# Layer 0 keeps the split projection weights of the first half in DRAM for the second half

## The chip, the cores and the metric

The kernel runs on one core of one Trainium2 chip. The metric is device time in microseconds (us) from the start to the end of one execution. Engines are named as in the profile: PE is TensorE, DVE is VectorE, ACT is ScalarE, POOL is GpSimd, SP is SyncE, which here issues nearly all transfers.

## The reference

The reference is a trunk of two layers over a sequence of 1024 steps and 1024 channels in float32. Layer 0 mixes with two head groups (RWKV-7, and a gated DeltaNet "gdn"), layer 1 with chunked attention; each layer then has an MLP and a gated embedding. The change touches only the input projection of layer 0:

```python
h = rmsnorm(x, norm_mix_g[i])
proj = h @ even_w_in[e]                     # 1024 x (3*512 + 4*512 + 8)
y_a, v_first = rwkv7_group(h, dh, proj[..., :o_ak], ...)   # r, k, v
y_b = gdn_group(proj[..., o_bq:o_bg], ...)                  # q, k, v, gate, two logits
mix = jnp.concatenate([y_a, y_b], -1) @ even_w_out[e]
```

## The kernel before

**Products in three parts.** A float32 product is made of three products in the format float32r: each operand is split into a high part (a cast by ScalarE, line L306) and a low part (a subtraction by VectorE, L307), and `mm3` multiplies high by high, high by low and low by high. One projection of 128 output channels for half of the sequence (512 steps) takes eight k-tiles, so 24 products of 128x512, written to a PSUM bank called `dps` and scaled out of it by VectorE (L684, L709 for LoRA).

**Weights.** The 28 blocks of the projection's weights (512 KB each) lie in `w_in`. `load_w` takes a raw buffer (tag `wraw`, two buffers), loads a block into it (L300, on SP's queue), and `split_w` splits it into a pair `whi`, `wlo` (two pairs). So a block may be loaded when the split before the last is done, and be split when the projection before the last has been multiplied.

**Units and lanes.** Layer 0 goes through the sequence in two halves (`hf` 0 and 1), each with eight units: four pairs of RWKV heads and four gdn heads in turn. A unit takes three weight blocks (RWKV) or four (gdn, the fourth is the gate). Each half begins with further products: the decay LoRA before the first unit's projections in the second half, and after the first unit the logits (`gdn_logits`, L719 and L720: a memset by GpSimd of a raw buffer, a small load, a split) and the gate LoRA (`lora`, L695 to L713). These use the same raw buffers and pairs.

Seven generators ("lanes") emit the instructions: the input lane `l0_in` makes projections, others the fronts (RWKV or gdn: VectorE, ScalarE and GpSimd work, then the start of a triangular inverse), the mids (the end of the inverse, banks `iz`), the backs (the recurrence over chunks, banks `ch`, `py`, `po`, `pm`) and the posts. A planner with a table of latencies chooses the lane that goes next; the projections fill the time in which the others wait. It counts products only, no loads and no splits. The order within an engine's queue is settled when the program is built, by when each instruction's operands and buffers are expected, and on the chip each queue is taken in order.

**The inverse's way through memory.** `inverse_start` stores a block matrix to DRAM (L399), loads it in another layout (L403), runs some 30 small operations on GpSimd (L411 to L421), stores the result (L423) and loads it again (L425). All four are on SP's queue, among the weight loads.

Of the kernel before, what the change touches and what calls it, by code (L numbers as in the profile page):

```python
# [8 lines left out]
F32 = mybir.dt.float32  # L9
F32R = mybir.dt.float32r  # L10
# [7 lines left out]
P = 128  # L18
T = 1024
# [93 lines left out]
class Trunk:  # L113
# [456 lines left out]
    def l0_in(self, units):  # L570
        nc, a, fr = self.nc, self.a, self.fr
        self.state = {}
        self.xg = []
        for u, (nm, p, hf) in enumerate(units):
            if u % 8 == 0:


                self.xg, squares = [], []
                if hf == 0:
                    acc = fr.tile([P, HB], F32, tag="rsbc", name="acc", bufs=2)  # L580
                    raw = self.wp.tile([P, 1024], F32, tag="wraw", name="wraw")
                    self.w_first = [self.wp.tile([P, 1024], F32R, tag=f"w{q}", name=f"w{q}") for q in ("hi", "lo")]
                    first = iter([slice(0, HB), slice(HB, T)])
                else:

                    x2 = [self.load_x(q, self.pre if q < 2 else self.wp, "ph" if q == 0 else "pl" if q == 1 else "wraw")
                          for q in range(4)]
                for k in range(NK):
                    if hf == 0:
                        if k % 2 == 0 and k < 4:  # L590
                            c = next(first)
                            nc.sync.dma_start(out=raw[:, c], in_=a["w_in"][4][:, c])
                            self.split_w(raw[:, c], HB, [z[:, c] for z in self.w_first])
                        xr = self.t2()
                        (nc.sync if k > 1 else nc.scalar).dma_start(out=xr, in_=a["x"][k, :, 0:HB])
                    else:
                        xr = x2[k // 2][:, k % 2, :]
                    if k % 2 == 0:
                        xg2 = self.pair(k // 2)
                    xg = xg2[:, k % 2]  # L600
                    self.split_scaled(xg, xr, self.vec("mixg", k), slice(0, HB))
                    self.xg.append(xg)
                    if hf == 0:
                        squares.append(lambda k=k, xr=xr: self.square(acc, xr, k == 0))
                for f in squares:
                    f()
                sc = {}
                if hf == 0:
                    rsc = self.sm.tile([P, 4], F32, tag="rsc", name="rsc")
                    self.rs = fr.tile([P, HB], F32, tag="rsbc", name="rsbc", bufs=2)  # L610

                    self.extra = [lambda t=t: self.psm.tile([P, HB], F32, tag=t, name="dps") for t in ("y", "ch", "pm")]
                    self.late, self.plan = [], {2: lambda: self.row_stats([acc], rsc), 3: lambda: self.to_rows(rsc, self.rs)}
                    raws = yield from getattr(self, nm + "_in")(p, hf, u)
                    self.wa2 = fr.tile([P, 512], F32, tag="wa2", name="wa2")
                    nc.sync.dma_start(out=self.wa2, in_=a["wa2"])
                    self.g2 = self.l0.tile([P, 512], F32, tag="g2", name="g2")
                    nc.sync.dma_start(out=self.g2, in_=a["g2"])
                    self.hv = self.l0.tile([P, 2, 4], F32, tag="hv", name="hv")
                    nc.sync.dma_start(out=self.hv.rearrange("p a b -> p (a b)"),  # L620
                                      in_=a["gdnhv"].rearrange("(o c) -> o c", o=1).broadcast_to((P, 8)))
                    self.ea = self.l0.tile([P, 1, 4], F32, tag="ea", name="ea")
                    nc.scalar.activation(self.ea, self.hv[:, 0:1, :], AF.Exp)
                    acc = fr.tile([P, HB], F32, tag="rsbc", name="acc", bufs=2)
                    for q in range(4):
                        x2 = self.load_x(q, self.pre, "pl" if q % 2 else "ph")
                        for e in range(2):
                            self.square(acc, x2[:, e], q + e == 0, nc.vector)
                else:
                    self.rs = acc  # L630
                self.pst = None
                sc["lwa"] = yield from self.lora(0, [(0, 64, 0), (64, 128, 1)], "la")
                nc.scalar.activation(sc["lwa"][0:64], sc["lwa"][0:64], AF.Tanh)
            if u:
                raws = yield from getattr(self, nm + "_in")(p, hf, u)
            self.state[u] = (raws, sc)
            self.mark(("in", u), 1.0)
            if u == 7:
                rsc = self.sm.tile([P, 4], F32, tag="rsc", name="rsc")
                self.row_stats([acc], rsc)  # L640
                yield "l0_in1"
                self.to_rows(rsc, acc)
            if u % 8 == 0:

                ba = yield from self.gdn_logits()
                gg = yield from self.lora(1, [(0, 128, 2)], "lg", lambda: self.gdn_scalars(hf, sc, ba))
                nc.scalar.activation(gg, gg, AF.Tanh, scale=0.5)
                nc.vector.tensor_scalar(gg, gg, 0.5, 0.5, op0=ALU.mult, op1=ALU.add)
                sc["lg"] = gg
                self.mark(("lg", hf))  # L650

        rsb = lambda: fr.tile([P, HB], F32, tag="rsbc", name="xs", bufs=2)
        pt = [self.pair(k) for k in range(2)]
        sc = [self.pair(q, F32) for q in (2, 3)]
        sc = [t[:, e] for t in sc for e in range(2)]
        yield from self.ple_proj(0, lambda k, hf: pt[k][:, hf], sc[0], lambda n: sc[1 + n % 3], rsb, self.load_w)
        yield from self.out_early(0, a["x"], self.pair, rsb, self.load_w, [("post", 7), ("post", 13), ("post", 14), ("post", 15)])
# [111 lines left out]
    def gdn_cum(self, sc):  # L769
# [16 lines left out]
        nc.scalar.activation(sc["ekd"], gl, AF.Exp)  # L786
        nc.scalar.activation(sc["egl"].rearrange("p i h -> p (i h)"), pc[:, 16:32], AF.Exp)

    def rwkv_in(self, p, hf, u):
        raws = []  # L790
        for j in (1, 0, 2):
            if u >= 2:
                yield ("raw", u - 2, j)
            w = self.load_w(self.a["w_in"][4 * j + p]) if u or j != 1 else self.w_first
            raws.append((yield from self.project(w, f"r{p}{j}", 1)))
        return [raws[1], raws[0], raws[2]]

    def gdn_in(self, n, hf, u):
        raws = []
        for j in (1, 0, 2):  # L800
            if u >= 2:
                yield ("raw", u - 2, j)
            raws.append((yield from self.project(self.load_w(self.a["w_in"][12 + 4 * j + n]), f"g{n}{j}", 3)))
        if u >= 4:
            yield ("front", u - 2)
        gate = yield from self.project(self.load_w(self.a["w_in"][24 + n]), None, 0, "gate")
        return [raws[1], raws[0], raws[2], gate]

    def rwkv_front(self, p, hf, sc, raws, u):
# [1376 lines left out]
```

## Time and profile before

| | us |
|---|---|
| median of 3 runs | 3078.52 |
| lowest and highest run | 3070.69, 3079.13 |
| the profiled execution, whole | 3086.63 |
| its span, first to last instruction | 3084.8 |
| its mean granted TensorE clock | 0.974 of full |

The profile's page gives busy time by engine, then the span in 40 slices, the DMA queues, the chain that ended last, and the costliest groups of instructions, as line, engine, operation, output<-input, count, busy time and mean, and the idle time before them with its releaser. The windows view gives the same busy times for chosen stretches. In the timeline the first two columns are start and duration in us; a bracket at the end holds the idle time of the engine before it and what ended it. A row `A <- B: t, n, m` of the waits says that A waited for B for t us in all, n times, at most m us.

The first half of layer 0 lies at about 0 to 415 us of the span, the second at about 415 to 790 us.

### The profile page before, as it was taken

To read this page: it belongs to the slowest core of one execution; us is meant where nothing else is said; L and a number is where in the kernel's file an instruction comes from. 1 tells how busy PE (TensorE), PEld (TensorE's weight loads), DVE (VectorE), ACT (ScalarE), POOL (GpSimd) and SP (SyncE) were. 2 spreads that over 40 slices of the span, in tenths; PEclk is the share of its full clock that TensorE was granted. 3 is DMA by queue.
4 is the path that set the end of the run, shared out by engine and by line. 5 is a ranking of instruction groups with operands and counts; after the bars stand their busy time and mean duration, and the time that the engine had idled before them with its cause. 6 is when DMAs were issued, how large, how long until landed. Compare 5 with 4: busy or idle time off the path is not lost.

```text
span 3084.8 us, 47290 instructions
## 1 busy us (share of the span) xinstructions
PE 2970.1 (96%) x17254; PEld 2457.1 (80%) x17254; DVE 2209.9 (72%) x4546; ACT 1486.2 (48%) x2957; POOL 552.9 (18%) x985
## 2 busy tenths in 40 slices
PE   8999999999999999999999999999999999999999
PEld 6777777777777888788887988898878888888887
DVE  7556766667758777788887676676768777788883
ACT  4333433434437555544444465565757555544441
POOL 5434442443500000000005111111210000000002
PEclk9899999999999999999999999999999999999999
DMA  4212112212346444754424211110256444654433
GB/s 145 64 55 62 54 49 75 61 55 68 110 157 227 162 150 151 262 166 151 151 95 131 70 44 40 43 61 23 75 181 223 163 154 153 237 190 150 150 103 116
DMA packets 194857, 368.49 MB, mean 119 GB/s; under 512 B 46800, under 2 KB 49088, under 8 KB 194624
## 3 DMA queue, kind: packets, MB, share of 16 engines
q1 hardware_dynamic: 163808, 309.35, 31.4%
q10 hardware_dynamic: 30816, 56.11, 4.7%
q8 instruction: 136, 2.23, 0.3%
q14 instruction: 97, 0.79, 0.1%
HBM read 268.86 MB, written 96.53 MB: 118 GB/s over the span
## 4 chain that ended last, share of the span: by engine, by line
PE 71%; DVE 14%; DMA 6%; ACT 4%; issue 2%; POOL 1%; SPq 0%; ACTq 0%; DVEq 0%; POOLq 0%
PE dps L180 57%; PE ch L180 2%; PE po L180 2%; DVE act L1283 2%; PE pm L180 1%; PE iz L180 1%; PE pt L195 1%; DMA late<-in_w 1%; PE sn L180 1%; PE tp L180 1%; DMA late<-hd 1%; DVE late L1431 1%; DMA wraw<-in_w_out 1%; PE py L180 1%; DVE wlo L307 1%
## 5 line engine op out<-in xcount | busy, mean ns | idle before, releaser
L180 PE MATMUL dps<-r,act 128*128 128x512 f32 x3720 | 872.9, 392 | 2.0 <-DVE xw L1550 0.8
L180 PEld LDWEIGHTS dps<-r,act 128*128 128x128 f32 x3720 | 698.0, 188 | 157.0 <-issue 1.2
L180 PE MATMUL dps<-xg,whi 128*128 128x512 f32 x1280 | 436.0, 421 | 11.2 <-ACT whi L306 7.4
L1647 POOL TENSOR_TENSOR pn<-pn,prs 128x512 f32<-128x512 f32 x32 | 47.3, 1483 | 1542.6 <-ACT prs L389 1419.5
L180 PE MATMUL dps<-wq,act 128*128 128x384 f32 x1536 | 307.8, 347 | 13.8 <-DVE vs L1909 6.0
L180 PEld LDWEIGHTS dps<-xg,whi 128*128 128x128 f32 x1280 | 236.2, 197 | 62.2 <-ACT whi L306 7.6
L180 PEld LDWEIGHTS dps<-wq,act 128*128 128x128 f32 x1536 | 269.6, 193 | 17.7 <-DVE vs L1909 7.6
L180 PE MATMUL dps<-xg,wlo 128*128 128x512 f32 x640 | 260.7, 407 | 2.6 <-DVE wlo L307 2.6
L1282 ACT CAST act<-act 128x512 fp32r<-128x512 f32 (+2 forms) x281 | 159.3, 600 | 142.0 <-PE dps L180 59.8
L1283 DVE TENSOR_TENSOR act<-act 128x512 fp32r<-128x512 f32 (+2 forms) x281 | 180.1, 669 | 4.6 <-ACT act L1282 4.6
L180 PE MATMUL dps<-act 128*128 128x512 f32 x720 | 176.5, 393 | 2.0 <-DVE late L1404 2.0
L1282 ACT CAST act<-late 128x512 fp32r<-128x512 f32 x210 | 123.7, 620 | 100.4 <-PE dps L180 73.8
L180 PE MATMUL dps<-late,act 128*128 128x512 f32 x672 | 166.6, 392 | 0.0
L180 PEld LDWEIGHTS dps<-act 128*128 128x128 f32 x720 | 136.2, 189 | 32.1 <-DVE late L1404 2.4
L1283 DVE TENSOR_TENSOR act<-late,act 128x512 fp32r<-128x512 f32 x210 | 139.1, 687 | 31.1 <-ACT act L1282 30.9
L180 PEld LDWEIGHTS dps<-xg,wlo 128*128 128x128 f32 x640 | 125.0, 195 | 32.5 <-DVE wlo L307 3.8
L180 PEld LDWEIGHTS dps<-late,act 128*128 128x128 f32 x672 | 126.0, 188 | 27.7
L180 PE MATMUL dps<-xw,act 128*128 128x512 f32 x576 | 145.9, 392 | 0.2 <-ACT act L1282 0.2
L1550 DVE TENSOR_TENSOR xw<-xw,dps 128x512 f32<-128x512 f32 x192 | 130.0, 682 | 17.3 <-PE dps L180 17.2
L306 ACT CAST whi<-wraw 128x1024 fp32r<-128x1024 f32 (+1 forms) x79 | 81.8, 1035 | 107.6 <-PE dps L180 77.1
L180 PEld LDWEIGHTS dps<-xw,act 128*128 128x128 f32 x576 | 107.9, 188 | 24.4 <-ACT act L1282 0.7
L180 PE MATMUL po<-ptile,vs 128*128 128x256 f32 (+1 forms) x576 | 106.8, 295 | 15.5 <-ACT ptile L352 9.7
(488 smaller groups left out, 5600.7 us busy)
## 6 DMA issues: line engine op xcount, KB each, us to landing
hb<-late ACTq DMA_DIRECT2D x196, 256.0 KB
act<-hb SPq DMA_DIRECT2D x158, 256.0 KB
late<-in_w SPq DMA_DIRECT2D x60, 512.0 KB
act<-in_w SPq DMA_DIRECT2D x112, 256.0 KB
wraw<-in_w_in SPq DMA_DIRECT2D x55, 512.0 KB
braw<-hb SPq DMA_DIRECT2D x80, 256.0 KB
wraw<-in_w_out SPq DMA_DIRECT2D x21, 512.0 KB
wraw<-in_w_qkv SPq DMA_DIRECT2D x21, 512.0 KB
```

The lines of the kernel that those rows point to most:

```text
L180: return self.begin(self.nc.tensor.matmul(out, lhsT, rhs, start=start, stop=stop, skip_group_check=again))
L195: return self.begin(self.nc.tensor.transpose(out, in_, ident))
L306: nc.scalar.copy(hi, raw)
L307: nc.vector.tensor_tensor(lo, raw, hi.bitcast(F32), op=ALU.subtract)
L1282: A.copy(hi, s)
L1283: V.tensor_tensor(lo, s, hi.bitcast(F32), op=ALU.subtract)
L1431: V.tensor_tensor(t, u, v, op=ALU.subtract)
L1550: V.tensor_tensor(x[n][:, hs[hf]], x[n][:, hs[hf]], ps, op=ALU.add)
L1647: G.tensor_tensor(pn, pn, prs[:, sl], op=ALU.mult)
```

## The change

In the first half `load_in` loads and splits each block as before, and then stores its high and low part to DRAM (two stores of 512 KB on SP's queue, into the tensors `wd`). The block that the kernel splits ahead of everything (`w_first`, block 4) is stored within `l0_in`. In the second half `load_in` loads both parts in place of the raw block; there is no split. Two of three blocks go into the `whi`, `wlo` pairs, and every third into the two raw buffers (`nw % 3 == 2`), which no projection's raw block needs in that half. The loads wait on nothing but a free buffer and the stores of the first half. LoRA, logit and all later weights are loaded and split as before.

```diff
     def l0_in(self, units):
...
+        self.wd, self.nw = {}, -1
...
                             self.split_w(raw[:, c], HB, [z[:, c] for z in self.w_first])
+                            if k == 2:
+                                self.wd[4] = [self.dr.tile([P, T], F32, tag=f"wd4{q}", name="wd") for q in "hl"]
+                                for d, z in zip(self.wd[4], self.w_first):
+                                    nc.sync.dma_start(out=d, in_=z.bitcast(F32))
...
+    def load_in(self, o, hf):
+
+        nc = self.nc
+        if hf == 0:
+            hi, lo = w = self.load_w(self.a["w_in"][o])
+            self.wd[o] = [self.dr.tile([P, T], F32, tag=f"wd{o}{q}", name="wd") for q in "hl"]
+            for d, z in zip(self.wd[o], w):
+                nc.sync.dma_start(out=d, in_=z.bitcast(F32))
+            return w
+        self.nw += 1
+        if self.nw % 3 == 2:
+            w = [self.wp.tile([P, T], F32R, tag="wraw", name="w" + q) for q in ("hi", "lo")]
+        else:
+            w = [self.wp.tile([P, T], F32R, tag=f"w{q}", name=f"w{q}") for q in ("hi", "lo")]
+        for d, z in zip(self.wd[o], w):
+            nc.sync.dma_start(out=z.bitcast(F32), in_=d)
+        return w
+
     def rwkv_in(self, p, hf, u):
...
-            w = self.load_w(self.a["w_in"][4 * j + p]) if u or j != 1 else self.w_first
+            w = self.load_in(4 * j + p, hf) if u or j != 1 else self.w_first
...
     def gdn_in(self, n, hf, u):
...
-            raws.append((yield from self.project(self.load_w(self.a["w_in"][12 + 4 * j + n]), f"g{n}{j}", 3)))
+            raws.append((yield from self.project(self.load_in(12 + 4 * j + n, hf), f"g{n}{j}", 3)))
...
-        gate = yield from self.project(self.load_w(self.a["w_in"][24 + n]), None, 0, "gate")
+        gate = yield from self.project(self.load_in(24 + n, hf), None, 0, "gate")
```

## The prediction

> **What bounds the kernel now.** I read the page first, then the busy time of each engine in the two halves of layer 0, then the groups of instructions in the second half, the waits of TensorE there, and the timelines around TensorE's gaps.
>
> ```profile
> span 3084.8 us, 47290 instructions
> PE 2970.1 (96%) x17254; PEld 2457.1 (80%) x17254; DVE 2209.9 (72%) x4546; ACT 1486.2 (48%) x2957; POOL 552.9 (18%) x985
> PEclk9899999999999999999999999999999999999999
> ```
>
> TensorE is busy for 96% of the span, so what this change can win is idle TensorE time and time at a lowered clock, and only where the removed work stood: the second half of layer 0, about 415 to 790 us. The windows view gives those stages (microseconds; busy time and count of PE, PEld, DVE, ACT, POOL; then the granted clock, the DMA share and GB/s):
>
> ```profile
> 77.00:410.00 333.00, 319.09 (x2747) 245.67 (x2746) 208.69 (x464) 126.35 (x262) 141.47 (x320) 0.93 0.21 60
> 415.00:790.00 375.00, 360.78 (x3070) 278.07 (x3069) 240.67 (x568) 144.30 (x308) 154.78 (x360) 0.96 0.20 61
> 10.00:15.00 5.00, 4.37 (x16) 3.16 (x15) 4.11 (x6) 5.00 (x10) 4.80 (x11) 1.00 1.04 400
> 450.00:455.00 5.00, 5.00 (x56) 3.70 (x55) 4.28 (x10) 0.00 (x0) 3.19 (x7) 0.50 0.14 58
> ```
>
> In the second half TensorE stands idle for 375 - 360.78 = 14.2 us, and a clock of 0.96 over 375 us loses another 15 us. So 29 us (0.95% of the span) is the most that can be won there, if every stall went.
>
> **What is removed.** The 28 projection weights of the second half lose a ScalarE cast and a VectorE subtraction each. The groups of instructions by line in that stage (busy us, mean ns, idle before and its cause; 32 and 31 because LoRA and logit weights are split there too, and stay so):
>
> ```profile
> L307 DVE TENSOR_TENSOR wlo<-wraw,whi 128x1024 fp32r<-128x1024 f32 x31 | 39.4, 1272 | 3.5 <-ACT whi L306 3.4
> L306 ACT CAST whi<-wraw 128x1024 fp32r<-128x1024 f32 x32 | 33.5, 1046 | 34.7 <-PE dps L180 32.0 <-DMA wraw<-in_w_ple 2.3 <-POOL subt L418 0.3
> ```
>
> That is 28 x 1.272 = 35.6 us of VectorE and 28 x 1.046 = 29.3 us of ScalarE, and most of the 32.0 us in which ScalarE stood at a cast until TensorE released a buffer. But neither engine is the bound. What TensorE waits for there, and its larger gaps (last bracket: idle time, releaser):
>
> ```profile
> PE pm L180 <- DVE PMQ L942: 5.4, 3, 2.9
> PE tp L180 <- DVE b L875: 2.9, 2, 1.5
> 449.66 1.65 PE L180 MATMUL pm<-AR,b 64*128 64x128 f32 x4 [2.03 <-DVE PMQ L942]
> 573.04 1.16 PE L180 MATMUL tp<-AR,b 64*128 64x128 f32 x16 [1.40 <-DVE b L875]
> 576.20 1.62 PE L180 MATMUL pm<-AR,b 64*128 64x128 f32 x4 [1.07 <-POOL subt L418]
> 664.92 1.22 PE L180 MATMUL pm<-AR,b 64*128 64x128 f32 x3 [2.90 <-DVE PMQ L942]
> 761.12 1.16 PE L180 MATMUL tp<-AR,b 64*128 64x128 f32 x16 [1.52 <-DVE b L875]
> ```
>
> These four places make 8.9 of the 14.2 us, and no wait for a projection's weights is among them. Each is the RWKV front's own VectorE chain. VectorE ahead of the last gap, and the one split that stands ahead of the first:
>
> ```profile
> 757.90 1.58 DVE L901 SCALAR_TENSOR_TENSOR f<-f,vecs 128x512 f32<-128x512 f32 x1
> 759.40 0.68 DVE L684 TENSOR_TENSOR raw<-dps,acc 128x512 f32<-128x512 f32 x1
> 760.00 1.06 DVE L875 TENSOR_TENSOR b<-f 128x512 f32<-128x512 f32 x1
> 762.06 1.21 DVE L307 TENSOR_TENSOR wlo<-wraw,whi 128x1024 fp32r<-128x1024 f32 x1
> 444.74 1.20 DVE L307 TENSOR_TENSOR wlo<-wraw,whi 128x1024 fp32r<-128x1024 f32 x1
> ```
>
> At 761 the split comes after the operation awaited; the one at 444.74 belongs to the gate LoRA, which keeps its split. So the relief is far nearer to nothing than to 29: bounds 0 and -29 us. I take **-3 us**, a tenth, for shorter VectorE queues elsewhere.
>
> **What is added in steady state.** A second-half load is now two transfers of 512 KB each into the buffers that the products read. I price it by SyncE's issue, the 400 GB/s of the window 10:15 above, and the longest wait for a small transfer to land:
>
> ```profile
> wraw<-in_w_in SPq DMA_DIRECT2D x55, 512.0 KB
> L300 SPq DMA_DIRECT2D wraw<-in_w_in x55: 327/333/530, 6.6 to 738.4; - x55
> SPq L425 <- DMA z<-sub: 11.2, 8, 2.4
> SPq L399 <- DVE b L1119: 53.1, 5, 17.0
> ```
>
> 1.05 MB at 400 GB/s is 2.6 us; with 0.33 us of a second issue and 2.4 us it is 5.3 us from release to use. There are three buffer pairs (two of their own, and the raw pair for every third weight), so weight n may load once projection n-3 has been multiplied, and must be there when n-1 has. VectorE's evictions show the ends of projections; the two shortest such spans I found:
>
> ```profile
> 475.57 0.69 DVE L709 TENSOR_TENSOR lgo<-dps,acc 128x512 f32<-128x512 f32 x1 [0.15 <-PE dps L180]
> 485.65 0.69 DVE L684 TENSOR_TENSOR raw<-dps,acc 128x512 f32<-128x512 f32 x1 [0.15 <-PE dps L180]
> 513.57 0.69 DVE L684 TENSOR_TENSOR raw<-dps,acc 128x512 f32<-128x512 f32 x1 [8.55 <-PE dps L180]
> 523.43 0.69 DVE L684 TENSOR_TENSOR gate<-dps,acc 128x512 f32<-128x512 f32 x1 [1.92 <-PE dps L180]
> ```
>
> They are 10.1 and 9.9 us long, so a load of 5.3 us is covered, unless SyncE then stands at a wait of its own: it stood at the store that starts an inverse (L399) for up to 17.0 us. A load caught behind all of that is late by 17.0 + 5.3 - 9.9 = 12.4 us. I take **0**, upper end +12. The wait for the pair itself moves from ScalarE to SyncE; behind it there stand later loads and the stores and loads of the inverse.
>
> In the first half, SyncE gets two stores behind each split. They become ready at the moment when the load after next does (that load waits for the same split), so they add two issues (0.66 us), no new long wait. Their 28 x 1.05 = 29.4 MB take 73 us at 400 GB/s out of 333, so the DMA share goes from 0.21 to about 0.43. An inverse goes through memory in four hops (store, load, store, load): 8 x 4 hops, each meeting stores with a chance of about 0.2 and then waiting half of 2.6 us on average, make 8 us in all. No row of TensorE's waits above names a transfer, so I take **+1**, ends 0 and +8. The stores can't speed the first half up, as nothing is taken from it.
>
> **At the start** the transfers are saturated (share 1.04 above), and the first LoRA load is the next thing due:
>
> ```profile
> 18.41 0.34 SPq L695 DMA_DIRECT2D lraw<-in_lora  x1
> 24.45 2.05 POOL L703 TENSOR_TENSOR wraw<-lraw,d_omul 128x512 f32<-128x512 f32 x2
> 26.54 1.05 ACT L306 CAST whi<-wraw 128x1024 fp32r<-128x1024 f32 x1 [6.57 <-POOL wraw L703]
> ```
>
> Issued at 18.41, it needs 2.4 + 1.3 us, so it is there by 22.1, and GpSimd uses it at 24.45. Three stores ahead of it (1.57 MB, 3.9 us) would make that 26.0: 1.6 us late. I take **+0.5**, ends 0 and +2.
>
> **Between the halves.** The logit weights (L719) use a raw buffer. It used to be free as soon as a split was done; now the third projection of the first second-half unit holds both raw buffers until its last product. GpSimd, SyncE, TensorE and VectorE there:
>
> ```profile
> 419.01 0.94 POOL L719 MEMSET wraw<- 128x1024 f32 x1
> 419.98 0.60 SPq L720 DMA_DIRECT2D wraw<-in_wba  x1
> 423.78 0.50 POOL L411 TENSOR_SCALAR_AFFINE_SELECT sub<-subb 32x256 f32<-32x256 f32 x1 [3.70 <-DMA subb<-scr]
> 437.20 0.65 POOL L421 COPY sub<-sub 32x256 f32<-32x256 f32 x1
> 441.76 0.62 PE L180 MATMUL dps<-xg,whi 128*128 128x512 f32 x2
> 442.86 0.69 DVE L684 TENSOR_TENSOR raw<-dps,acc 128x512 f32<-128x512 f32 x1
> 443.33 0.25 PE L180 MATMUL iz<-T,Ng 32*32 32x16 f32 x8
> ```
>
> The third projection is evicted at 442.86, its buffers come free at about 442. Memset 0.94, issue 0.60, landing 2.4, cast 1.05 and subtraction 1.27 follow: 6.3 us, to about 448.3. The logit products began at 441.76. If TensorE keeps its order it waits 6.3 us; the gap of 2.03 us at 449.66 then goes, since VectorE catches up meanwhile: 4.3 us. A halved clock comes on top: behind the 2.03 us gap TensorE ran at 0.50 for 5 us, which costs 2.5 us. That gives +6.8. If the inverse and recurrence products are put ahead of the logits instead, the 2.03 us gap takes up the logits and it costs nothing. Queue orders are set when the program is built, by when operands are expected, so the second is likely in part: **+3**, ends 0 and +7.
>
> The Trainium skill ("TensorE: Matmul & The Clock Gate", Part 1) says that the clock halves after an idle window of about 3.4 us. The row 450:455 differs: 2.03 us idle was enough. By the page shorter waits would cost no clock, the half-way value would be 2 rather than 3, and the sum below +0.5.
>
> **Sum.** -3 + 0 + 1 + 0.5 + 3 = **+1.5 us**. The profiled execution took 3086.6 us (span 3084.8), 8 us over the median of 3078.5; so 3088.1 for it and **3080.0** beside the median. With ends that rarely meet, this case spans about -8 to +9 us.
>
> **Rivals.** *Slower, the memset in GpSimd's way.* GpSimd takes its queue in order. If the memset keeps its place ahead of the inverse's operations (419.01 before 423.78), the inverse starts after about 443 and not at 423.78: 19 us late. TensorE's first inverse product, at 443.33, then waits about 19 us, less the 2.03 us gap: +17, so 3080 - 3 + 17 = 3094. It decides if L719 stands ahead of L411 in GpSimd's queue. For it: that order is there now. Against: the memset's readiness is known when the order is made. *Slower, the hops.* All 8 us of waiting hops show: 3080 + 7 = 3087, with a late load or the start's upper end 3090. The Trainium skill ("DMA: Bandwidth & Descriptors", Queues, rings and completion order) says that each DMA engine takes one queue's work in ring order, which is this rival's mechanism; no run here shows it yet. Against it: no TensorE wait for a transfer. *Faster.* Freed ScalarE and VectorE shorten the recurrence, and half of the 29 us goes: -14.5 + 4.5 = -10, 3068.5. For it: ScalarE's 32.0 us at the casts. Against: no gap above has a removed split in front of it.
>
> **How the numbers follow.** A measurement of this kernel can tell about 0.3% (9 us) from no change. Forecast 0.44, which lies within 0.3%; memset 0.18, slower; hops and late loads 0.18, about the bound, of which I count 0.15 slower and 0.03 same; faster 0.20. So faster 0.20, same 0.47, slower 0.33. The range runs from 3066 (a little beyond the faster case) to 3098 (the memset case with a late start); 0.2 is left out. The forecast's own range is 3072 to 3089.
>
> **What would show it.** Casts at L306 in the second half fall from 32 to 4, and ScalarE's wait at them from 32 us to little; the four gaps stay; written bytes rise by 29 MB, the first half's DMA share to about 0.43; L719 starts at 442 or later. I am wrong if the RWKV front's gaps go (faster), if GpSimd waits at L719 with the inverse behind it, or if TensorE waits for a weight's transfer (slower).

## The result

| | before | after |
|---|---|---|
| median (runs) | 3076.15 us (22) | 3068.52 us (22) |
| lowest and highest run | 3067.63, 3085.11 | 3055.84, 3075.47 |
| the profiled execution, whole | 3086.63 | 3072.22 |
| its span | 3084.8 | 3070.2 |
| its mean granted TensorE clock | 0.974 | 0.980 |

The ratio is 0.9976 [0.9966, 0.9986]: 7.6 us between the medians, 7.4 by the ratio. The interval excludes no change, so the kernel is a little faster; the size stays inside the 0.3% that the prediction had named. The spans of the two profiled executions lie 14.6 us apart, twice the medians' difference, so differences of single profiles are read with care below.

The page of the kernel after, its heads:

```profile
span 3070.2 us, 47342 instructions
PE 2960.9 (96%) x17254; PEld 2448.3 (80%) x17254; DVE 2167.2 (71%) x4518; ACT 1459.8 (48%) x2929; POOL 540.4 (18%) x985
HBM read 283.54 MB, written 125.89 MB: 133 GB/s over the span
```

VectorE lost 28 instructions (4546 to 4518) and 42.7 us of busy time, ScalarE 28 and 26.4 us. The windows of the first and the second half (columns as in the prediction):

```profile
77.00:410.00 333.00, 317.46 (x2695) 244.42 (x2694) 205.13 (x460) 124.15 (x257) 141.05 (x319) 0.92 0.39 134
415.00:790.00 375.00, 365.99 (x3206) 282.47 (x3199) 213.84 (x567) 122.72 (x291) 140.44 (x360) 0.99 0.33 104
```

In the second half TensorE is idle for 375 - 365.99 = 9.0 us, where it was 14.2, and its clock is 0.99, where it was 0.96. The first half gained nothing. (A window of fixed time holds more work in the faster kernel, 3206 products and not 3070; a stretch of fixed work follows with the table of all runs.) Groups by line in the second half, and what TensorE waits for there:

```profile
L307 DVE TENSOR_TENSOR wlo<-wraw,whi 128x1024 fp32r<-128x1024 f32 x5 | 6.1, 1225 | 3.6 <-ACT whi L306 3.6
L306 ACT CAST whi<-wraw 128x1024 fp32r<-128x1024 f32 x5 | 5.2, 1046 | 7.5 <-POOL wraw L708 3.6 <-DMA z<-sub 1.3 <-PE dps L180 1.0
```

```profile
PE tp L180 <- DVE b L898: 2.2, 2, 1.4
PE ch L180 <- ACT W L997: 1.9, 1, 1.9
PE dps L180 <- ACT whi L306: 1.5, 2, 0.9
PE pm L180 <- DVE PMQ L965: 0.9, 1, 0.9
```

The casts are gone but for five, and with them ScalarE's 32.0 us of waiting for TensorE in front of them (1.0 is left). The wait for `PMQ` fell from 5.4 to 0.9 us. No wait for a weight's transfer has come in its place. TensorE's larger gaps there (last bracket: idle time, releaser):

```profile
451.60 0.73 PE L180 MATMUL dps<-xg,whi 128*128 128x512 f32 x2 [0.60 <-ACT whi L306]
570.26 0.66 PE L180 MATMUL ch<-W,F 128*128 128x64 f32 x4 [1.94 <-ACT W L997]
571.77 2.08 PE L180 MATMUL tp<-AR,b 64*128 64x128 f32 x16 [0.85 <-DVE b L898]
656.70 0.92 PE L180 MATMUL pm<-AR,b 64*128 64x128 f32 x4 [0.89 <-DVE PMQ L965]
749.33 1.16 PE L180 MATMUL tp<-AR,b 64*128 64x128 f32 x16 [1.40 <-DVE b L898]
```

The largest gap of before, 2.90 us at 664.92, is 0.89 us here. VectorE's timeline shows why, before and then after:

```profile
659.16 1.76 DVE L874 SCALAR_TENSOR_TENSOR AR<-f,E 128x512 f32<-128x512 f32 x1
660.84 1.75 DVE L818 SCALAR_TENSOR_TENSOR f<-raw,vecs,f 128x512 f32<-128x512 f32 x1
662.70 1.70 DVE L901 SCALAR_TENSOR_TENSOR f<-f,vecs 128x512 f32<-128x512 f32 x1
664.32 0.54 DVE L942 TENSOR_TENSOR PMQ<-pm,mask 128x384 f32<-128x384 f32 x1
```

```profile
654.42 1.76 DVE L897 SCALAR_TENSOR_TENSOR AR<-f,E 128x512 f32<-128x512 f32 x1
656.10 0.55 DVE L965 TENSOR_TENSOR PMQ<-pm,mask 128x384 f32<-128x384 f32 x1
656.76 1.10 DVE L841 SCALAR_TENSOR_TENSOR f<-raw,vecs,f 128x512 f32<-128x512 f32 x1
```

Before, `PMQ` stood in VectorE's queue behind two operations of 1.75 and 1.70 us; after, it stands right behind `AR`. No split was taken out between them: the queues were written in another order when the program was built. TensorE's queue holds some 14,800 matrix instructions; set side by side as the programs are built, the two written orders differ in some 1,500 lines (buffer numbers left out; a row that moved counts twice, also where the expectations below speak of rows), some 340 of them in layer 1, more than half in its attention, which the change does not touch.

So there are two theories. **Engine time**: 28 x 1.27 us of VectorE and 28 x 1.05 us of ScalarE less in the second half let the queues serve TensorE earlier, in whatever order they are written. **Order**: any edit makes a new order, and this one came out well.

### The profile page after: what moved, and what is told of

Read it like the earlier page. It is cut to its first block, busy times and chain, and to the rows that moved or that the text cites. A ratio compares the mean times of both kernels' runs of the same rounds, so it can differ in the third digit from the quotient of the medians.

```text
span 3070.2 us, 47342 instructions
## 1 busy us (share of the span) xinstructions
PE 2960.9 (96%) x17254; PEld 2448.3 (80%) x17254; DVE 2167.2 (71%) x4518; ACT 1459.8 (48%) x2929; POOL 540.4 (18%) x985
## 4 chain that ended last, share of the span: by engine, by line
PE 76%; DVE 11%; DMA 5%; ACT 3%; POOL 2%; issue 2%; SPq 0%; ACTq 0%; DVEq 0%; POOLq 0%
PE dps L180 62%; PE ch L180 2%; PE po L180 2%; PE iz L180 1%; PE pt L195 1%; PE pm L180 1%; PE tp L180 1%; PE sn L180 1%; DVE act L1306 1%; DMA late<-hd 1%; DMA wraw<-in_w_qkv 1%; PE py L180 1%; DVE ptile L353 1%; PE pp L180 1%; DVE pb L2047 0%
## 5 line engine op out<-in xcount | busy, mean ns | idle before, releaser
L180 PE MATMUL dps<-xg,whi 128*128 128x512 f32 x1280 | 429.5, 416 | 12.7 <-ACT whi L306 8.9
L1573 DVE TENSOR_TENSOR xw<-xw,dps 128x512 f32<-128x512 f32 x192 | 130.1, 682 | 18.3 <-PE dps L180 18.0
L180 PEld LDWEIGHTS po<-ptile,vs 128*128 128x128 f32 x576 | 87.1, 197 | 23.8 <-ACT ptile L352 13.5
```

Of the source, the lines that this page charges most:

```text
L180: return self.begin(self.nc.tensor.matmul(out, lhsT, rhs, start=start, stop=stop, skip_group_check=again))
L1573: V.tensor_tensor(x[n][:, hs[hf]], x[n][:, hs[hf]], ps, op=ALU.add)
```

## The experiments

### The change in parts

**Stores alone** (second half as before), **loads alone** (every block of the second half loads the stored pair of block 4, so that half multiplies by block 4's weights throughout; nothing else is stored), and the change **without the third pair** in the raw buffers.

```diff
 # stores alone, in place of the second half's branch of load_in
+        return self.load_w(self.a["w_in"][o])
 # loads alone
         if hf == 0:
+            return self.load_w(self.a["w_in"][o])
...
+        for d, z in zip(self.wd[4], w):
 # without the third pair
-        self.nw += 1
-        if self.nw % 3 == 2:
-            w = [self.wp.tile([P, T], F32R, tag="wraw", name="w" + q) for q in ("hi", "lo")]
-        else:
-            w = ...
+        w = [self.wp.tile([P, T], F32R, tag=f"w{q}", name=f"w{q}") for q in ("hi", "lo")]
```

Stores alone. 

> Only the first half's stores; the second half loads and splits raw weights as before. Freed engines (the gain comes from ScalarE and VectorE work that is gone): +1 to +5 us over before, all of it before 415 us, as the profile of the changed kernel is 3.3 us late at the first eviction of the second half. Fresh queue order (any change rebuilds the order of every queue, and this one happened to fall well): as likely faster as slower, by up to 8 us, and the difference lies in the second half too.

Loads alone. 

> Only the second half's loads: one stored pair (block 4's) is loaded for every projection there, the other 27 blocks are not stored, so the second half multiplies by block 4's weights throughout. Freed engines: -9 to -13 us against before, that is the changed kernel's -7.6 less the stores' cost, so that this and the stores alone add up to it within 3 us. Fresh queue order: no such sum; anything from -8 to +8.

Without the third pair. 

> The changed kernel without its third buffer pair: every second-half load goes to the two pairs, so block n loads when projection n-2 has been multiplied. If the gain is freed VectorE and ScalarE time: -4 to -8 us against before, near the changed kernel's -7.6, as a load of 5.3 us still fits a projection of 5.7 us or more. If the early loads make the gain: lost, 0 to +8 us, with TensorE waiting for loads of whi and wlo.

Measured: stores alone 0.9993 [0.9979, 1.0006], loads alone 0.9961 [0.9945, 0.9977], without the third pair 0.9981 [0.9964, 0.9998]. The stores cost nothing that can be measured, the gain lies with the loads, and the third pair is not needed for a gain in the ratio. But the parts do not add up: -2.2 and -12.0 us make -14, the whole change has -7.4, and the expectation had allowed 3 us. The order of layer 1, below, is the likely reason.

**Half a split.** The stored high part and the raw block are loaded and VectorE still subtracts (no cast), or the stored low part and the raw block and ScalarE still casts (no subtraction); both with two pairs.

```diff
+        raw = self.wp.tile([P, T], F32, tag="wraw", name="wraw")
+        nc.sync.dma_start(out=raw, in_=self.a["w_in"][o])
+        hi, lo = w = [self.wp.tile([P, T], F32R, tag=f"w{q}", name=f"w{q}") for q in ("hi", "lo")]
+        nc.sync.dma_start(out=hi.bitcast(F32), in_=self.wd[o][0])     # no cast
+        nc.vector.tensor_tensor(lo, raw, hi.bitcast(F32), op=ALU.subtract)
 # or
+        nc.sync.dma_start(out=lo.bitcast(F32), in_=self.wd[o][1])     # no subtraction
+        nc.scalar.copy(hi, raw)
```

> Stores kept; the second half loads the raw block and the stored high part, and VectorE still subtracts: only ScalarE's casts go (two buffer pairs). Freed ScalarE (its wait of 32 us at the casts blocks the recurrence): most of the changed kernel's gain stays, -4 to -8 us. Freed VectorE: the gain is lost, 0 to +4 us.

> Stores kept; the second half loads the raw block and the stored low part, and ScalarE still casts: only VectorE's subtractions go (two buffer pairs). Freed VectorE (TensorE waited for it in nearly all gaps of the second half): -4 to -8 us. Freed ScalarE: 0 to +4 us.

Without the cast 1.0042 [1.0025, 1.0060], without the subtraction 0.9987 [0.9974, 1.0001]. Taking the cast alone away is worse than taking nothing away. TensorE's waits in the second half name VectorE (`U` and `S` belong to the recurrence):

```profile
PE ch L180 <- DVE U L1003: 6.7, 6, 2.0
PE ch L180 <- DVE S L1019: 3.6, 2, 3.3
```

Whether VectorE's new wait for two transfers does that was not tried by itself. With only the subtraction gone the interval reaches no change.

**LoRA and logit weights as well.** Their pairs are stored and loaded too, so the last splits go.

> The changed kernel, with the same done to the LoRA and logit weights: their five split pairs are stored in the first half and loaded in the second, which drops 5 casts, 5 subtractions, GpSimd's scalings of the LoRA weights and the memset there. If freed time on VectorE, ScalarE and GpSimd shortens the second half: -3 to -6 us beyond the changed kernel, -10 to -14 against before. If the 28 blocks were enough, or the place between the halves isn't on the path: -5 to -9.

0.9988 [0.9969, 1.0007]: no more is gained. Its second half is about as long as with the splits (table below) and its layer 1 is written in an order of its own; why stays open.

### Engine time put back

**A first try missed its place.** The changed kernel with three idle subtractions per block on VectorE, or three idle copies on ScalarE, reading `g2`, a constant.

```diff
+        for _ in range(3):
+            nc.vector.tensor_tensor(self.dum, self.g2[:, 0:320], self.g2[:, 0:320], op=ALU.subtract)
 # or
+            nc.scalar.copy(self.dum, self.g2[:, 0:224])
```

> The changed kernel with idle work put back on VectorE only: three subtractions of 128x320 into a spare tile per second-half block (about 1.3 us, as much as the split took). They wait for nothing. Freed VectorE time: the gain goes, -2 to +4 us against before. Freed ScalarE, or the wait at the casts: the gain stays, -5 to -9.

> The changed kernel with idle work put back on ScalarE only: three copies of 128x224 into a spare tile per second-half block (about 1.05 us). They wait for nothing. Freed VectorE time: the gain stays, -5 to -9 us against before. Freed ScalarE time: -2 to +4. Wait at the casts rather than their time: the gain stays here too, and in the run with VectorE's idle work.

1.0062 [1.0041, 1.0082] and 0.9992 [0.9973, 1.0012]. Neither tells what it was meant to: since the work waits for nothing but a constant, it was placed far ahead of its loads. The row of the idle tile on VectorE (duration min/median/max in ns, first and last start), and the first 77 us of that kernel:

```profile
L812 DVE TENSOR_TENSOR dum<-g x84: 443/491/1579, 18.8 to 107.7; 128x320 fp32r<-128x320 f32 x84
```

```profile
0.00:77.00 77.00, 55.51 (x205) 42.02 (x206) 64.54 (x110) 31.77 (x49) 45.50 (x101) 0.89 0.53 186
```

TensorE is busy for 55.5 us there, at a clock of 0.89, and in the changed kernel for 62.2 at 0.96:

```profile
0.00:77.00 77.00, 62.24 (x271) 47.00 (x272) 50.22 (x102) 37.70 (x64) 46.51 (x105) 0.96 0.61 213
```

The last gate of the first half comes at 398.2 us, where the changed kernel's two profiles have 380.5 and 372.4. In this order VectorE's time at the start costs far more than in the second half. Both runs stay of use, since their second half holds none of the idle work.

**Tied to the loads.** The same amounts, reading the parts just loaded.

```diff
+        hi, lo = [z.bitcast(F32) for z in w]
+        for c in range(3):
+            nc.vector.tensor_tensor(self.dum, hi[:, c * 320:c * 320 + 320], lo[:, c * 320:c * 320 + 320], op=ALU.subtract)
 # or
+            nc.scalar.copy(self.dum, w[0].bitcast(F32)[:, c * 224:c * 224 + 224])
```

> The changed kernel, with three 128x320 subtractions on VectorE for each of the 28 blocks of the second half, of the parts just loaded and into a tile that nobody reads: about the 1.47 us of VectorE that the change took out for each block, and tied this time to the load, so that they stand in the second half. Freed VectorE time: the gain goes, 3076 to 3082 us, 0.9 % of VectorE's row of the second half comes back as about 41 us of busy time, and the stretch between the last gates of the two halves is 407 to 414 us again. Freed ScalarE time or a ScalarE wait: stays at 3067 to 3071, stretch 396 to 403. A fresh order of the queues: anything from 3060 to 3080, without relation to the busy time.

> The changed kernel, with three 128x224 copies on ScalarE for each of the 28 blocks of the second half, of the high part just loaded and into a tile that nobody reads: about the 1.1 us of ScalarE that the change took out for each block, tied to the load. Freed ScalarE time: the gain goes, 3074 to 3080 us, and the stretch between the last gates of the two halves is 405 to 414. Freed VectorE time: 3066 to 3071, stretch 396 to 403. A fresh order of the queues: 3060 to 3080, without relation to the busy time.

1.0005 [0.9991, 1.0018] on VectorE and 1.0018 [1.0004, 1.0033] on ScalarE. The gain is gone in both. The second half with VectorE's work put back, then with ScalarE's:

```profile
415.00:790.00 375.00, 361.50 (x3134) 278.64 (x3129) 246.60 (x617) 118.79 (x278) 145.86 (x359) 0.97 0.31 101
```

```profile
415.00:790.00 375.00, 360.90 (x3033) 277.07 (x3030) 203.18 (x523) 141.69 (x347) 137.87 (x356) 0.96 0.31 98
```

TensorE is idle for 13.5 and 14.1 us again, with only one of the two engines as busy as before. But VectorE also stood waiting for loads in front of this work:

```profile
L813 DVE TENSOR_TENSOR dum<-whi,wlo x84: 434/492/1478, 393.5 to 736.8; 128x320 fp32r<-128x320 f32 x84
...
  DMA wlo<-wd: 31.6, 22
```

So the next run reads the pair loaded before, which was expected to have landed long since (the same three subtractions, on `self.prev`).

> The changed kernel with three 128x320 subtractions on VectorE for each of the second half's blocks but the first, as in the earlier run with idle subtractions, but of the pair loaded before, which has landed long since: the same work without its waits for a load. Freed VectorE time: the gain stays lost, 3074 to 3082 us, ratio 0.999 to 1.002. If only the waits for the load in VectorE's queue had eaten the gain: back to 3066 to 3071, ratio 0.9966 to 0.9986.

0.9994 [0.9980, 1.0008]: the gain stays lost. But the waits did not go, so this run alone does not tell the work from the waits: VectorE still stood for 29.2 us at a load, 21 times, where it was 31.6 and 22. What tells them apart is the version with 128x8 subtractions of the same pair, further below: it waits at least as long, has a tenth of the work, and keeps its gain. The rows of the idle tile in the two, and in front of what they waited:

```profile
L815 DVE TENSOR_TENSOR dum<-whi,wlo x81: 432/492/1472, 397.2 to 737.2; 128x320 fp32r<-128x320 f32 x81
...
  DMA wlo<-wd: 29.2, 21
```

```profile
L815 DVE TENSOR_TENSOR dum<-whi,wlo x27: 149/167/259, 398.4 to 731.1; 128x8 fp32r<-128x8 f32 x27
...
  DMA wlo<-wd: 35.0, 16
```

So those waits are not what loses the gain; what is left is VectorE's work and the order that is written with it. No such pair was run on ScalarE, whose idle copies waited 49.3 us for loads.

### Order changed with next to no work

Two loads of 128x4 words that nobody reads, in the kernel before and in the changed one:

```diff
+            if u in (3, 11):
+                spare = self.sm.tile([P, 4], F32, tag="spare", name="spare")
+                nc.sync.dma_start(out=spare, in_=a["vecs"][:, 0:4])
```

> The kernel before, with one load of 128x4 words that nobody reads, at the fourth and at the twelfth unit: as work this is nothing, but the order in which every queue of the kernel is written out comes from a calculation over all its steps and may come out another way. If the order moves the time by itself as much as the change did, this is 5 to 10 us away from the kernel before (ratio under 0.9985 or over 1.0015). If the change's gain is that of its freed engine time, this is within 3 us of the kernel before, and the stretch between the last gates of the halves is 409 to 415.

> The changed kernel with the same two loads that nobody reads. If the gain is that of the freed engine time: 0.9966 to 0.9986 of the kernel before, as without them, stretch between the last gates of the halves 394 to 400. If it is an accident of the order: anywhere from 0.995 to 1.003, and the stretch may be 405 or more.

0.9997 [0.9979, 1.0015] and 0.9989 [0.9976, 1.0002]. In the kernel before the edit moved no row of TensorE's, VectorE's, ScalarE's or GpSimd's queues, so this run is the kernel before once more. In the changed kernel it makes some 1,100 lines of difference in TensorE's, 250 of them in layer 0, its stretch (404.3 us) falls between the two expectations, and its interval reaches from the changed kernel's ratio to no change. Then one subtraction of 128x8 for each block of the second half (of the pair just split, or of the pair loaded before):

```diff
+            self.nc.vector.tensor_tensor(self.dum, hi.bitcast(F32)[:, 0:8], lo.bitcast(F32)[:, 0:8], op=ALU.subtract)
```

In the kernel before: 

> The kernel before, with one 128x8 subtraction on VectorE for each of the second half's 28 blocks, into a tile that nobody reads: about 28 times 0.06 us of work, but the order in which the queues are written out comes out otherwise (270 of some 14,800 rows of TensorE's queue stand elsewhere). Freed engine time as the cause: ratio 0.9985 to 1.0015. Order as the cause: 3 us or more away, either way.

In the changed kernel: 

> The changed kernel, with one 128x8 subtraction on VectorE of the pair loaded before, for each of the second half's blocks but the first: some 1.7 us of work and another written order (376 rows of TensorE's queue). Freed engine time as the cause: the gain stays, ratio 0.9966 to 0.9986. Order as the cause: a ratio outside that, up to 1.001.

1.0015 [1.0003, 1.0026] and 0.9956 [0.9941, 0.9971]. The order matters too, on the scale of the change: some 4.6 us to the worse in one, some 6 us to the better in the other. (A subtraction of 128x8 took 0.17 us here and not 0.06, so 27 of them are 4.5 us of VectorE.) Next the changed kernel with the stores of the high parts on ScalarE's queue, which leaves the order of TensorE and VectorE as it is:

```diff
-            for d, z in zip(self.wd[o], w):
-                nc.sync.dma_start(out=d, in_=z.bitcast(F32))
+            for eng, d, z in zip((nc.scalar, nc.sync), self.wd[o], w):
+                eng.dma_start(out=d, in_=z.bitcast(F32))
```

> The changed kernel, with the stores of the high parts issued by ScalarE right behind the cast that makes them, instead of on SP's queue, where the changed kernel's stores waited 113 us for casts with later loads behind them; low parts as before on SP's queue. The order on TensorE and VectorE is unchanged. If the stores cost the first half something by these waits (the version with loads alone gained 12 us, the changed kernel 7): 3063 to 3067 us, ratio 0.995 to 0.997. If they cost nothing, as the version with stores alone has it: ratio 0.9966 to 0.9986. If ScalarE's issuing costs more than it frees: 3072 to 3078.

0.9995 [0.9982, 1.0007]: no gain by the other queue, and the changed kernel's own gain not to be seen, though its second half looks like the changed kernel's (table below). To tell scatter from order, the changed kernel and the one with the 128x8 subtractions ran again, side by side on one chip.

> The changed kernel itself, on the same chip and beside the next one. Freed engine time and a gain that stands: ratio 0.9966 to 0.9986 again, stretch between the last gates of the halves 394 to 400 us. If the order with the stores split over two queues (0.9995, the same order on TensorE and VectorE) showed the kernel's own scatter between chips and not the cost of another queue: up to 0.9995.

> The changed kernel with the 128x8 subtraction for each block, a second time and beside the changed kernel on the same chip. Its order on TensorE in layer 0 is that of the changed kernel but for 4 rows, and differs in the attention of layer 1, which the change doesn't touch. If the order of layer 1 makes its 0.9956: 0.001 to 0.003 below the changed kernel's ratio again, and the stretch of layer 1's products with the attention weights (558.5 us in the changed kernel, 552.8 with this order) 4 to 7 us shorter. If it was scatter: the two ratios agree within 0.001.

The changed kernel came to 0.9988 [0.9975, 1.0002], the other to 0.9963 [0.9944, 0.9983] (medians 3072.07 and 3062.69 us beside 3076.42 of before). The 0.9956 was no scatter: the second value lies 0.0025 below the changed kernel's beside it. The three ratios of the changed kernel's order (0.9976, 0.9988, and 0.9995 with the split stores) spread over 6 us; whether the other queue has a part in that stays open. TensorE's orders in the two differ by 4 lines in layer 0, and by some 380 in layer 1. In its attention, the products with the attention weights (row: first and last start) and the wait for `pb`, in the changed kernel's second profile and then in the other's:

```profile
L180 PE MATMUL po<-ptile,vs x576: 219/279/582, 1737.0 to 2300.3; 128*128 128x256 f32 x144, 128*128 128x128 f32 x48
```

```profile
PE pt L195 <- ACT pb L2057: 5.9, 4, 2.8
```

```profile
L180 PE MATMUL po<-ptile,vs x576: 219/279/562, 1734.3 to 2287.9; 128*128 128x256 f32 x144, 128*128 128x128 f32 x48
```

```profile
PE pt L195 <- ACT pb L2064: 3.1, 3, 1.2
```

That stretch takes 563.3 us in the one order (558.5 in the first profile, 561.3 with the split stores) and 553.6 in the other (552.8 in its first profile, 553.0 in loads alone, 557.4 in stores alone, which both have the same order there). On average that is some 7 us, in a layer that was not edited, and the two ratios differ by 0.0020 and 0.0025, 6 to 8 us. The version with the idle subtraction is the fastest complete kernel here, by an accident of its order. The stretch alone does not price an order: it is 561.2 us in the kernel before, which is no slower beyond the interval than stores alone with 557.4.

### All runs in one table

"Stretch" goes from the last gate eviction of the first half to that of the second. "Way" is a stretch of nearly fixed work: from VectorE's eviction of the second half's decay LoRA (`lao`) to the end of the recurrence's last product on TensorE (into `ch`); it holds 4,197 to 4,219 products (4,165 in the first row with VectorE's time put back). "Idle" is TensorE's on the way. All three come from one profile each. The last column names the written order of layer 1: equal letters are equal orders, a dash is an order of its own; a* differs from a by 8 lines, e* from e by 60.

| splits in the second half | ratio | stretch us | way us | idle us | layer 1 |
|---|---|---|---|---|---|
| there: before | 1 | 412.5 | 519.4 | 20.4 | a |
| before, two tiny loads | 0.9997 | 413.2 | 520.2 | 22.3 | a |
| before, 128x8 | 1.0015 | 412.3 | 517.7 | 19.0 | c |
| stores alone | 0.9993 | 413.5 | 521.5 | 19.8 | b |
| gone, time put back: VectorE | 1.0005 | 406.8 | 519.0 | 22.3 | a* |
| ScalarE | 1.0018 | 409.9 | 521.1 | 18.3 | - |
| VectorE, pair loaded before | 0.9994 | 411.2 | 522.0 | 18.1 | a* |
| gone: after | 0.9976 | 396.6 | 504.9 | 13.1 | d |
| after, again | 0.9988 | 400.3 | 512.2 | 12.8 | d |
| stores on two queues | 0.9995 | 403.1 | 512.5 | 13.2 | d |
| two tiny loads | 0.9989 | 404.3 | 515.3 | 12.7 | e |
| 128x8 | 0.9956 | 401.5 | 511.4 | 15.3 | b |
| 128x8, again | 0.9963 | 400.4 | 511.4 | 13.9 | b |
| loads alone | 0.9961 | 396.2 | 508.0 | 12.5 | b |
| gone, idle work at the start: VectorE | 1.0062 | 403.4 | 511.4 | 13.1 | - |
| ScalarE | 0.9992 | 402.8 | 515.1 | 13.6 | c |
| LoRA and logits too | 0.9988 | 405.9 | 518.1 | 21.2 | - |
| without the third pair | 0.9981 | 412.5 | 520.2 | 12.9 | c |
| half there: casts gone | 1.0042 | 422.3 | 526.7 | 24.2 | - |
| subtractions gone | 0.9987 | 407.4 | 516.0 | 18.2 | e* |

The way, for before and for after, and then for ScalarE's time put back in the second half and at the start (columns as before; the products and TensorE's busy time give the idle time):

```profile
398.78:918.20 519.42, 499.02 (x4216) 385.92 (x4215) 337.83 (x769) 197.02 (x412) 195.28 (x425) 0.95 0.25 79
402.07:907.00 504.93, 491.85 (x4216) 381.08 (x4215) 298.39 (x742) 170.11 (x384) 182.97 (x425) 0.98 0.34 111
391.01:912.10 521.09, 502.81 (x4197) 388.26 (x4198) 299.78 (x742) 199.08 (x468) 182.85 (x425) 0.95 0.33 107
403.70:918.80 515.10, 501.50 (x4216) 387.78 (x4216) 299.04 (x741) 169.79 (x384) 183.51 (x425) 0.96 0.33 109
```

The rows of the stretch, for before and for after:

```profile
L684 DVE TENSOR_TENSOR gate<-dps,rsbc x4: 678/688/692, 107.0 to 377.0; 128x512 f32<-128x512 f32 x4
L684 DVE TENSOR_TENSOR gate<-dps,acc x4: 678/692/693, 523.4 to 789.5; 128x512 f32<-128x512 f32 x4
```

```profile
L689 DVE TENSOR_TENSOR gate<-dps,rsbc x4: 684/688/693, 101.2 to 380.5; 128x512 f32<-128x512 f32 x4
L689 DVE TENSOR_TENSOR gate<-dps,acc x4: 682/688/692, 518.3 to 777.1; 128x512 f32<-128x512 f32 x4
```

On the way no two groups overlap where it matters. With the splits it is 517.7 to 521.5 us; with the time put back in the second half 519.0 to 522.0; with three pairs and no time put back there 504.9 to 515.3, in nine runs (the seven from "after" to "loads alone" and the two with idle work at the start). TensorE's idle time agrees: 19.0 to 22.3, 18.1 to 22.3, and 12.5 to 15.3 us. The stretch between gates shows the same gain, but only a part of its loss (406.8 to 411.2 with the time put back).

The orders of layer 0 behind the nine runs are six, of which two differ by 4 lines only and the others by 150 to 640; those behind the four runs with splits are really two, since the first three differ by at most 8 lines, and stores alone from them by over 900. So the freed time gains in the second half in every order that was tried, and put back there on either engine it loses the gain. Is it the work itself, or the order that is written with it? For ScalarE the runs speak for the work. The version with its copies in the second half differs in layer 0 by some 110 lines from loads alone, and by as many from the version with the same copies at the start; loads alone differs from the changed kernel by over 300. Yet the way is 521.1 us in the first and 504.9 to 515.1 in the three others. For VectorE the order with the work put back lies some 970 lines from the changed kernel's, so there the two can't be told apart.

Three runs do not fit. Without the third pair the idle time and the ratio are as with the splits gone, the way and the stretch as with the splits there; with LoRA and logits too, the way and the idle time are as with the splits there; that was one profile each and stays open. With the casts gone it is worse than with nothing gone.

The order of layer 1 comes on top, so ratios are best compared where it is equal. Order b: stores alone 0.9993 against loads alone and 128x8 (0.9961, 0.9956, 0.9963), 0.0033, about 10 us. Order c: 128x8 in the kernel before 1.0015 against two pairs 0.9981, 0.0034 (and 0.9992 with ScalarE's idle work at the start). Order a: before (1, 0.9997) against VectorE's time put back (1.0005, 0.9994), nothing. The changed kernel's own ratios, 0.9976 and 0.9988, would be the gain of 10 us less what its order of layer 1, d, gives back; no kernel with the splits has that order, so this last step is inferred.

## Why the prediction was wrong

The forecast was +1.5 us, 3080.0 beside a median of 3078.5; the rival "faster" with 3068.5 is what came, at -7.4.

**The step that failed is the relief.** It was put at -3 of 29 us. On the way of the table, the seven runs with three pairs and no idle work of size (from "after" to "loads alone") take 510.8 us on average against 519.7 in the four with the splits: -8.9, of which -7.0 is TensorE's idle time (13.4 against 20.4) and the rest busy time, where a lowered clock shows. The pairs with an equal order of layer 1 say 10 us. That is three times the forecast, and a third of the 29 us; the rival had half. The bound of 29 us was itself too narrow: it stops at 790 us, but the recurrence of the second half runs on to 918 us, and on that way TensorE is idle for 20.4 us and a clock of 0.95 loses another 26.

Why a tenth: the argument that no removed split stands in front of a gap read one written order as if it stayed. But the order comes from when operands are expected, so with 65 us of work taken from two engines another one is written, and `PMQ` at 664.92 lost its 3.45 us of unrelated work in front of it. The prediction itself used that the order is set when the program is built, for the memset, and did not use it for the gaps. That the gaps stay was wrong accordingly: the two for `PMQ` nearly went (2.03 at 449.66, 2.90 at 664.92), the two for `b` stayed (0.85 and 1.40 after). The prediction also counted five rows as four places, all of the front's VectorE chain; the fifth, 1.07 us at 576.20, waited for GpSimd's `subt` of the inverse, and it went as well.

That the number came out so near the rival's is in part luck: the same kernel gave 0.9976 and 0.9988, and the order of layer 1 moved two kernels of nearly the same layer 0 by 6 to 8 us.

**Between the halves**, +3: not paid. The memset was written behind the inverse's operations and waited 3.25 us for its buffer, as the GpSimd rows show:

```profile
425.13 0.49 POOL L411 TENSOR_SCALAR_AFFINE_SELECT sub<-subb 32x256 f32<-32x256 f32 x1 [5.16 <-DMA subb<-scr]
437.06 0.64 POOL L421 COPY sub<-sub 32x256 f32<-32x256 f32 x1
445.30 0.95 POOL L724 MEMSET wraw<- 128x1024 f32 x1 [3.25 <-PE dps L180]
```

So the rival of the memset in GpSimd's way did not happen. Of the prediction's two cases it is the second that came, the one that costs nothing: TensorE's queue has the inverse's products ahead of the logits' (445.40 to 450.17, then 451.60). TensorE lost 0.60 us at the cast behind it (451.60 above). From the decay LoRA's eviction to the gate LoRA's it takes 72.6 us after and 76.8 before; over the seven runs it is 72.5 to 76.2, over the four with the splits 76.8 to 77.8, and the gap for `PMQ` at 449.66 lies within it, so the two terms can't be parted here:

```profile
398.78 0.69 DVE L709 TENSOR_TENSOR lao<-dps,acc 128x512 f32<-128x512 f32 x1 [0.26 <-PE dps L180]
```

```profile
402.07 0.69 DVE L714 TENSOR_TENSOR lao<-dps,acc 128x512 f32<-128x512 f32 x1
474.64 0.69 DVE L714 TENSOR_TENSOR lgo<-dps,acc 128x512 f32<-128x512 f32 x1
```

**First-half stores**, +1, and the **start**, +0.5: not contradicted, and too small to be measured: together 0.9993 [0.9979, 1.0006]. The written bytes rose from 96.53 by 29.36 MB, as forecast, and the DMA share to 0.39 (0.43 forecast). **Steady-state loads**, 0: right; no wait for them. SyncE takes over the waiting, and no wait of TensorE's names a transfer:

```profile
SPq L809 <- PE dps L180: 175.6, 25, 17.3
```

**The casts** fell from 32 to 5 (4 forecast), ScalarE's wait for TensorE at them from 32.0 us to 1.0.

What the sum left out is the order of layer 1: it had no term, and with 6 to 8 us between two orders of the same work there it is as large as the whole result.

## What to carry to other kernels

Where the order of the queues is computed when the program is built, a gap in the old profile is no fixed place: work taken from a busy engine anywhere in a stage can move what stands in front of another gap, so price the relief by the whole idle and clock loss of the stage, to its last product, and give a fifth to a third of it a good chance (here 9 of 46 us, or of the 29 that were counted). Before a difference of a few tenths of a per cent is put down to an edit, change the order with an edit that does no work, and compare kernels whose order is the same outside the edited stage. Idle work that is to stand at a place must depend on something that becomes ready there; look in its profile whether it stands there, and whether the waits that it was to avoid are gone. Compare stretches of equal work, not windows of equal time.

## What the runs showed of the hardware

Short gaps are followed by a lowered clock. In the kernel before, the 5 us windows behind the gaps of 2.03 us (450 us), of 1.40 and 1.07 us (575 us) and of 2.90 us (665 us) all show 0.50, and behind one of 1.52 us (765 us) 0.58. In the changed kernel's second profile the 5 us windows around 563 us, where the gaps of 1.94 and 0.85 us lie, show a clock of 0.94 and then 0.50 (columns: busy times and counts, clock, DMA share, GB/s):

```profile
560.00:565.00 5.00, 2.21 (x16) 1.41 (x15) 4.90 (x7) 0.78 (x2) 4.99 (x7) 0.94 0.63 210
565.00:570.00 5.00, 5.00 (x34) 3.92 (x35) 2.83 (x8) 2.18 (x8) 3.08 (x9) 0.50 0.09 21
```

TensorE was idle for 2.79 us of the first of them, in two pieces. At 0.50 the next 5 us do the work of 2.5, about 2.5 us lost on top of such a gap. The Trainium skill ("TensorE: Matmul & The Clock Gate", Part 1) gives an idle window of about 3.4 us for the halving; here the longest single gap ahead of it was 1.94 us, and the measurement decides.

VectorE's time has no fixed price. Some 40 us of idle subtractions in the second half made the way 519.0 and 522.0 us where it is 510.8 on average without them, 8 to 11 us more. At the start, where 27 of 47 us of them stood in the first 77 us, the second half's decay LoRA was evicted at 421.4 us, where the changed kernel's profiles have 402.1 and 391.8, 19 to 30 us later, and the ratio was 1.0062; each with the order that it made.
